# Fourier and hyena mixer products and filter spectra in one fp32 product on unsplit operands, with ordering conditions on the output products beside them

## The chip, the cores and the metric

The kernel runs on one core of one Trainium2 chip. The metric is the device time of one execution in microseconds (us), the median of several runs. TensorE does the matrix products (PE in the profile; its weight loads are PEld), VectorE (DVE) and ScalarE (ACT) the elementwise work, GpSimd (POOL) some of it, and SyncE (SP) issues most DMAs. Each engine executes its instructions in a fixed order.

## The reference, cut to what matters

The program computes two transformer layers, and then a further block with dilated and neighbourhood attention and a mixture of experts. Everything is fp32. The part that the change touches is in each of the two layers, on x (512 tokens) and, in layer 0 only, on the context c (256 tokens); width 1024, of which 512 go through attention, 256 through a Fourier mixer and 256 through a long convolution ("hyena"):

```
def fourier_mix(f, w):                       # f: B, L, 256 in 4 groups of 64
    y = jnp.fft.fft2(fg, axes=(1, 3), norm='ortho').real
    return y.reshape(B, L, FOURIER_W) @ w
def hyena_longconv(u, filt, bias):           # filt: 2L x 256, made by a small MLP, normalised
    uf = jnp.fft.rfft(u, n=2 * L, axis=1);  kf = jnp.fft.rfft(filt, n=2 * L, axis=0)
    y = jnp.fft.irfft(uf * kf[None], n=2 * L, axis=1)[:, :L]
    return y + u * bias
mix_x = jnp.concatenate([attn_x, four_x, hy_x], axis=-1) @ w_out[i]
```

The three FFTs (of the Fourier mixer, of the signal and of the filter) and the inverse one are products with tables of cosines and sines.

## The kernel before, in words

**The product in three.** Nearly all matrix products go through `mm3` (L306 to L312). Each operand is held as two tiles of the type fp32r, a high part and the rest, made by `split` (L334 to L338): ScalarE rounds into the high part (L337), VectorE or GpSimd subtracts (L338). `mm3` then issues three products: high times high (L310), high times low (L311), low times high (L312). In the trace each is one record. A few small products, the modulation vectors' (`mps`, L406) among them, take plain fp32 operands and are issued once; such a product shows as two records in the trace.

**The mixers.** `fourier` (from L1130) multiplies the 64-point table `bd` by the weight `wf` (tile `wps`, 4 products a layer), the strided columns of the signal `Fx` or `Fc` by that (`abps`, 512 columns each, 8 for x and 4 for c), and the result `ab` by the table `tf` (`yps`, 16 for x and 8 for c); VectorE adds the residues (`foac`, `foy`). `hyena` (from L1201) transposes the signal `u` (`utp`), multiplies by the table `hf` (`ups`, 8 for x, 4 for c), forms sums (`us`), multiplies by the filter's spectrum `kt` on VectorE and GpSimd, forms sums again (`zs`, then `zya` and `zyb`, which hold the spectrum Y), splits Y into `ys`, multiplies by the table `hi` (`iyp`, 16 for x, 8 for c) and scales and adds (`hyt`, L1305). In `yps` and `iyp` only 128 columns of most products are used; 256 are computed. Layer 0 thus has 4 + 12 + 24 + 12 + 24 = 76 such triple products, layer 1, without c, has 4 + 8 + 16 + 8 + 16 = 52.

**The filters.** `filters` (from L592) makes the filter of each layer and length. Its spectrum is `kps`, 40 triple products of 256 columns over the whole program (16 at the start, the others beside layer 0's attention), and an alternating sum `alt`, 20 products with four output rows.

**What sets the order.** The tile framework's scheduler writes a static order for each engine from the program and a model of times, so the code's generators give only a preference. `gated` (L509) adds a condition for that scheduler alone: an instruction is placed behind another; no semaphore comes of it. In layer 0 the Fourier mixer, hyena and `outA` (from L1506) are driven together: `outA` multiplies the attention's output `mixA` by the first half of `w_out` (tile `dps`, 4 blocks of x and 2 of c, 2 halves, 4 x 3 products each, so 144), writes it to DRAM (`yd`, L1518), from which it is read back as `y` (L1532). Then `outFH` multiplies the mixers' outputs (`mixF`, `mixH`) by the second half (again 144 products) and adds to `y`. The FFN follows. In layer 1 the mixers run beside the attention (`sps`, `ptp`, `po`), two steps of theirs to one of the attention.

**Loads.** The tables, and the signals that an earlier stage left in DRAM (`fd`), are loaded by `ldr` (L517) on GpSimd's queue, as fp32r; the signals of hyena (`u`, `x`, `x0uc`, L1209 to L1214) and the spectra `kt` by SP.

Of the kernel before, what the change touches and what calls it, by code (L numbers as in the profile page):

```python
# [27 lines left out]
def _split(v):  # L28
    v = np.asarray(v, np.float64)
    m, e = np.frexp(v)  # L30
    hi = np.ldexp(np.round(m * 4096.0) / 4096.0, e)
    r = v - hi
    m, e = np.frexp(r)
    lo = np.ldexp(np.round(m * 4096.0) / 4096.0, e)
    return hi.astype(np.float32), lo.astype(np.float32)


# [6 lines left out]
def consts():  # L44
# [17 lines left out]
    hf, hi = (np.stack(_split(np.stack(t, 1))).reshape(2, 128, 1024) for t in (hf, hi))  # L62
    c["hftab"], c["hitab"] = hf, hi
    tf = np.stack(_split(np.stack(tf, 1))).reshape(2, 128, 2, 768)
    c["ftab"] = tf.transpose(0, 2, 1, 3).reshape(4, 128, 768)
# [12 lines left out]
    c["bd64"] = np.stack(_split(bd), 0).transpose(2, 0, 1, 3).reshape(128, 512)  # L78
# [187 lines left out]
class Kern:  # L266
    def __init__(K, tc, A, off, out, dbg=None):
        K.tc, K.nc, K.A, K.off, K.out = tc, tc.nc, A, off, out
        K.dbg = dbg or {}
        K.n = 0  # L270
        K.bal = 0.0
        K.gate = None
        K.marks = []
# [76 lines left out]
    def setup(K):  # L350
# [11 lines left out]
        K.alt = K.cp.tile([128, 4, 4], F32R, name="alt")  # L362
        nc.vector.tensor_copy(K.alt.rearrange("p a b -> p (a b)"), K.sgn[:, 0:16])
# [228 lines left out]
    def filters(K, later, pg, hf=None):  # L592
# [21 lines left out]
        hf = list(hf or (K.ldr([128, 4, 2, 128], f"hf{p}", A["hftab"][p]) for p in range(2)))  # L614
        hn = pg([128, 2, 4, 1, 128], F32R, "hn")
        for p in range(2):
            nc.scalar.activation(hn[:, p, :, 0], hf[p][:, :, 1].bitcast(F32), AF.Copy, scale=-1.0)
            hf.append(hn[:, p])
# [21 lines left out]
    def filter(K, i, g, h2, w3, dec, hf):  # L640
# [4 lines left out]
        for b in range(nb):  # L645
            p3 = K.bank([128, 512], name="hp3")
            nc.tensor.matmul(p3, h2[:, b * 128:b * 128 + 128], w3, start=True, stop=True, tile_position=(64 * i, 0))
            fb = K.te([128, 2, 256], "hfb")
# [6 lines left out]
            kt = K.wlo([128, 2, 512], F32R, "kt")  # L655
            K.split(kt[:, 0], kt[:, 1], fb.rearrange("p a b -> p (a b)"))
# [4 lines left out]
            kts.append(kt)  # L661
# [76 lines left out]
    def mixer_in(K, i, pair, h, last, mods):  # L738
# [54 lines left out]
        for b in range(2):  # L793
            w = K.wk(K.wload(A["win"][i, 6 + b]), 128)
            for g in gs:
                n = 512 if g == "x" else 256
# [1 line left out]
                hi, lo = (K.te([128, 512], "fs", F32R)[:, :n] for p in range(2))
                K.split(hi, lo, ps)
                for p, t in enumerate((hi, lo)):  # L800
                    dst = K.fd[p, :, b * 512:b * 512 + 512] if g == "x" else K.fd[2, :, p * 512 + b * 256:p * 512 + b * 256 + 256]
                    nc.sync.dma_start(dst, t.bitcast(F32))
# [327 lines left out]
    def fourier(K, i, out, last, pg, t2):  # L1130

        nc, A = K.nc, K.A
        Fx = [K.ldr([128, 2, 512], f"Fx{p}", K.fd[p], pg) for p in range(2)]
        Fc = None if last else K.ldr([128, 2, 2, 256], "Fc", K.fd[2], pg)
        bd = K.ldr([128, 2, 2, 128], "bd", A["bd64"], pg)
        wf = t2([128, 2, 256], "wf")
        nc.sync.dma_start(wf.rearrange("p a b -> p (a b)"), A["wfour"][i])
        wr = pg([128, 2, 2, 256], F32R, "wr")
        K.split(wr[:, 0], wr[:, 1], wf)
        tf = [[K.ldr([128, 2, 384], f"tf{p}{j}", A["ftab"][2 * p + j], pg) for j in range(2)] for p in range(2)]  # L1140
        W = pg([128, 2, 512], F32R, "Wh"), pg([128, 2, 512], F32R, "Wl")
        for b in range(2):
            ps = K.bank([128, 2, 256], name="wps")
            for s in range(2):
                K.mm3(ps[:, s], (bd[:, 0, s], bd[:, 1, s]), (wr[:, 0, b], wr[:, 1, b]), True, True)
            ps = ps.rearrange("p a b -> p (a b)")
            K.split(W[0][:, b], W[1][:, b], ps)
        yield
        for g in (["x"] if last else ["x", "c"]):
            nb = 4 if g == "x" else 2  # L1150
            ab = []
            for r in range(nb):
                if r % 2 == 0:
# [1054 lines left out]
```

## Time and profile before

| | us |
|---|---|
| median of 3 runs | 2352.54 (2347.45 to 4198.28) |
| profiled execution, its own time | 2355.3 |
| its span | 2353.5 |
| TensorE busy | 2135.5 (91% of the span) |
| VectorE busy | 1522.3 (65%) |
| mean granted TensorE clock | 0.954 of full speed |

The stages in the span: the start with layer 0's filters and modulation to about 58 us, the input products to 170, attention 0 with the other filters to 362, the mixers of layer 0 with `outA` from 362 to 452.8, `outFH` to 485.5, then layer 0's FFN; attention 1 with layer 1's mixers from 1180 to 1321. The share of busy time is an average over all of these; what the change is worth is read from the stages that it touches, above all from the stretch from 362 to 453.

### The profile page before, as it was taken

The numbers are of one execution on the slowest core, as the hardware profiler recorded it, in microseconds if no ns is written. First come the engines' busy times: TensorE is split into PE (matmuls) and PEld (weight loads), VectorE is DVE, ScalarE is ACT, GpSimd is POOL, SyncE is SP. The second block draws the span as 40 slices with busy tenths as digits, with TensorE's granted clock in tenths as the row PEclk, the third lists the DMA queues.
The fourth block names the chain that finished last, engine by engine and source line by source line (L and its number), as shares of the span: only waits on it lengthen the run. The fifth ranks groups of instructions, "written<-read, shape, count | busy, mean of one in ns | idle before, by whom it ended". The sixth has DMA issues, their size and how long they took to land. (4 is left out here: it accounts for less than half of the span.)

```text
span 2353.5 us, 31469 instructions
## 1 busy us (share of the span) xinstructions
PE 2135.5 (91%) x11958; PEld 1744.1 (74%) x11958; DVE 1522.3 (65%) x2495; ACT 988.6 (42%) x1727; POOL 466.0 (20%) x448
## 2 busy tenths in 40 slices
PE   5899989679999999998987979999989999978895
PEld 2687678568888888886876768888867786756674
DVE  4744675777576777768557465555565645669895
ACT  3533663254322333235443444333344545347672
POOL 1410012221000000014213021000011212126743
PEclk9999999789999999999998989999999999979997
DMA  8363023623322344434130333222233335459993
GB/s 318 102 201 102 10 104 126 227 99 108 121 90 94 122 152 161 157 118 143 59 130 1 134 113 103 94 95 89 99 136 110 82 110 156 164 214 350 319 357 118
DMA packets 96991, 328.85 MB, mean 140 GB/s; under 512 B 11550, under 2 KB 12961, under 8 KB 96836
## 3 DMA queue, kind: packets, MB, share of 16 engines
q1 hardware_dynamic: 80176, 275.39, 33.0%
q0 software_dynamic: 14208, 42.48, 5.7%
q10 hardware_dynamic: 2452, 8.92, 0.9%
q8 instruction: 96, 1.57, 0.3%
q14 instruction: 59, 0.48, 0.1%
HBM read 285.68 MB, written 34.78 MB: 136 GB/s over the span
## 5 line engine op out<-in xcount | busy, mean ns | idle before, releaser
L328 DVE TENSOR_TENSOR wlo<-raw,whi 128x1024 fp32r<-128x1024 f32 x200 | 246.1, 1238 | 174.9 <-ACT whi L327 166.0
L327 ACT ACTIVATE whi<-raw 128x1024 fp32r<-128x1024 f32 x200 | 209.7, 1058 | 266.4 <-PE fps L311 196.6
L310 PE MATMUL fps<-h2x,whi 128*128 128x512 f32 x672 | 262.6, 392 | 4.0 <-DVE cvf L728 4.0
L311 PE MATMUL fps<-h2x,whi 128*128 128x512 f32 x672 | 263.0, 391 | 0.0
L312 PE MATMUL fps<-h2x,wlo 128*128 128x512 f32 x672 | 262.5, 391 | 0.0
L1413 POOL TENSOR_TENSOR cvf<-cvf 128x512 f32<-128x512 f32 x66 | 77.3, 1171 | 762.8 <-DVE cvf L728 681.9
L1336 DVE TENSOR_TENSOR y<-y,dps 128x512 f32<-128x512 f32 x200 | 134.2, 684 | 112.9 <-PE dps L312 112.4
L310 PEld LDWEIGHTS fps<-h2x,whi 128*128 128x128 f32 x672 | 126.5, 189 | 31.4 <-ACT whi L327 4.1
L312 PEld LDWEIGHTS fps<-h2x,wlo 128*128 128x128 f32 x672 | 126.9, 189 | 27.7 <-issue 1.6
L311 PEld LDWEIGHTS fps<-h2x,whi 128*128 128x128 f32 x672 | 127.0, 189 | 26.0 <-issue 0.4
L726 ACT ACTIVATE cvf<-fps,cv 128x512 f32<-128x512 f32 (+1 forms) x126 | 87.5, 695 | 138.6 <-PE fps L312 138.5
L311 PE MATMUL dps<-wlo,actx 128*128 128x512 f32 x352 | 137.1, 389 | 0.0
L310 PE MATMUL dps<-whi,actx 128*128 128x512 f32 x352 | 136.6, 390 | 0.3 <-DVE y L1336 0.3
L312 PE MATMUL dps<-whi,actx 128*128 128x512 f32 x352 | 136.3, 389 | 0.0
L429 DVE SCALAR_TENSOR_TENSOR ma<-wm,cs,ma 128x512 f32<-128x512 f32 x140 | 106.2, 803 | 19.3 <-DMA wm<-in_wmod 19.3
L310 PE MATMUL fps<-hx,whi 128*128 128x512 f32 x288 | 114.0, 396 | 0.5 <-ACT v L949 0.5
L312 PE MATMUL fps<-hx,wlo 128*128 128x512 f32 x288 | 113.3, 394 | 0.0
L311 PE MATMUL fps<-hx,whi 128*128 128x512 f32 x288 | 113.0, 392 | 0.0
L727 DVE SCALAR_TENSOR_TENSOR cvf<-fps,cv,cvf 128x511 f32<-128x511 f32 (+1 forms) x126 | 82.5, 655 | 30.5 <-ACT cvf L726 30.4
L310 PE MATMUL fps<-h2c,whi 128*128 128x256 f32 x336 | 96.3, 287 | 4.1 <-ACT cvf L726 4.1
L311 PE MATMUL fps<-h2c,whi 128*128 128x256 f32 x336 | 96.2, 286 | 0.0
L312 PE MATMUL fps<-h2c,wlo 128*128 128x256 f32 x336 | 96.2, 286 | 0.0
(630 smaller groups left out, 5514.5 us busy)
## 6 DMA issues: line engine op xcount, KB each, us to landing
wm<-in_wmod SPq DMA_DIRECT2D x96, 512.0 KB
raw<-in_wup SPq DMA_DIRECT2D x88, 512.0 KB
raw<-in_win SPq DMA_DIRECT2D x52, 512.0 KB
rawp<-in_wexp SPq DMA_DIRECT2D x48, 512.0 KB
raw<-in_wexp SPq DMA_DIRECT2D x48, 512.0 KB
raw<-in_wdown SPq DMA_DIRECT2D x44, 512.0 KB
raw<-in_wout SPq DMA_DIRECT2D x20, 512.0 KB
xd<-xt SPq DMA_DIRECT2D x20, 512.0 KB
```

Of the source, the lines that this page charges most:

```text
L310: mm(out, st[0], mv[0], start=start, stop=False)
L311: mm(out, st[0], mv[1], start=False, stop=False)
L312: K.lastmm = mm(out, st[1], mv[0], start=False, stop=stop)
L327: nc.scalar.activation(hi, raw, AF.Copy)
L328: (nc.gpsimd if pool else nc.vector).tensor_tensor(lo, raw, hi.bitcast(F32), op=ALU.subtract)
L429: o = nc.vector.scalar_tensor_tensor(a, v, c, a, op0=ALU.mult, op1=ALU.add)
L726: nc.scalar.activation(dst, ps, AF.Identity, scale=w[1], bias=w[3])
L727: nc.vector.scalar_tensor_tensor(dst[:, 1:n], ps[:, 0:n - 1], w[0], dst[:, 1:n], op0=ALU.mult, op1=ALU.add)
L1336: nc.vector.tensor_tensor(y[tb][:, c], y[tb][:, c], pss[hf], op=ALU.add)
L1413: nc.gpsimd.tensor_tensor(t[1], t[0], t[1], op=ALU.mult)
```

## The change

The Fourier and hyena products and the filter spectra are issued once each, in fp32, on unsplit operands (`mm1`, or `matmul` directly). The splits of those operands go: of `wf`, W, `ab`, `ut`, Y (the `ys` tiles), the filter (`kt`) and the signals (`fs`); where a copy from PSUM is still needed, one stays. The tables are held once instead of as two parts, and the loads of these operands move from GpSimd's queue to SP's (`ldf` for `ldr`). The columns that were computed and not used are dropped: `iyp` is 128 columns wide, `yps` 128 for c and for even residues of x. After it, layer 0 has 40 products of 128 columns, 24 of 256 and 12 of 512; layer 1 has 24, 20 and 8. The alternating sum takes four products at four column positions of the array. Last, in `outA`, the last product of each group is placed behind the mixer product that the program issued before the group began (`g = K.lastmm`, `K.gated(K.lastmm, g)`): a condition for the scheduler alone.

```diff
+    def mm1(K, out, st, mv, start, stop):
+        K.lastmm = K.nc.tensor.matmul(out, st, mv, start=start, stop=stop)
...
-    def ldr(K, shape, name, src, pg=None):
-
-        t = (pg or K.pg)(shape, F32R, name)
-        n = int(np.prod(shape[1:]))
-        flat = t if len(shape) == 2 else t.rearrange({3: "p a b -> p (a b)", 4: "p a b c -> p (a b c)", 5: "p a b c d -> p (a b c d)"}[len(shape)])
-        K.gated(K.nc.gpsimd.dma_start(flat, src))
+    def ldf(K, shape, name, src, pg=None):
+
+        t = (pg or K.pg)(shape, F32, name)
+        K.gated(K.nc.sync.dma_start(t if len(shape) == 2 else K.flat(t), src))
         return t
...
-            kt = K.wlo([128, 2, 512], F32R, "kt")
-            K.split(kt[:, 0], kt[:, 1], fb.rearrange("p a b -> p (a b)"))
...
-        alt = K.bank([128, 512], name="alt")[:nb]
+        alt = K.bank([128, 512], name="alt")
         for b, kt in enumerate(kts):
-            for z in range(2):
-                nc.tensor.matmul(alt, K.alt[:, b, :nb], kt[:, z], start=b == z == 0, stop=(b, z) == (nb - 1, 1))
-        ae = K.te([128, 512], "altr")[:nb]
-        nc.scalar.activation(ae, alt, AF.Copy)
+            nc.tensor.matmul(alt[32 * b:32 * b + 32], K.alt, kt.rearrange("p a b -> p (a b)"), start=True, stop=True, tile_position=(0, 32 * b))
+        ae = K.te([128, 512], "altr")[:32 * nb]
+        nc.scalar.activation(ae, alt[:32 * nb], AF.Copy)
...
-                    kv = tuple(kts[c][:, z, j * 256:j * 256 + 256] for z in range(2))
-                    K.mm3(ps[:, s], tuple(hf[z + 2 if t == 2 else z][:, c * (4 // nb), t % 2] for z in range(2)), kv, j == 0, j == 1)
+                    nc.tensor.matmul(ps[:, s], hf[t][:, c * (4 // nb)], kts[c][:, j], start=j == 0, stop=j == 1)
...
-        Fx = [K.ldr([128, 2, 512], f"Fx{p}", K.fd[p], pg) for p in range(2)]
-        Fc = None if last else K.ldr([128, 2, 2, 256], "Fc", K.fd[2], pg)
-        bd = K.ldr([128, 2, 2, 128], "bd", A["bd64"], pg)
-        wf = t2([128, 2, 256], "wf")
-        nc.sync.dma_start(wf.rearrange("p a b -> p (a b)"), A["wfour"][i])
-        wr = pg([128, 2, 2, 256], F32R, "wr")
-        K.split(wr[:, 0], wr[:, 1], wf)
-        tf = [[K.ldr([128, 2, 384], f"tf{p}{j}", A["ftab"][2 * p + j], pg) for j in range(2)] for p in range(2)]
-        W = pg([128, 2, 512], F32R, "Wh"), pg([128, 2, 512], F32R, "Wl")
+        Fx = K.ldf([128, 2, 512], "Fx", K.fd[0], pg)
+        bd = K.ldf([128, 2, 128], "bd", A["bd64"], lambda s, d, n: t2(s, n))
+        wf = K.ldf([128, 2, 256], "wf", A["wfour"][i], lambda s, d, n: t2(s, n))
+        Fc = None if last else K.ldf([128, 2, 256], "Fc", K.fd[2][:, 0:512], lambda s, d, n: pg([128, 4, 256], d, n)[:, 0:2])
+        tf = [K.ldf([128, 2, 384], f"tf{j}", A["ftab"][j], pg) for j in range(2)]
+        W = pg([128, 2, 512], F32, "W")
         for b in range(2):
             ps = K.bank([128, 2, 256], name="wps")
             for s in range(2):
-                K.mm3(ps[:, s], (bd[:, 0, s], bd[:, 1, s]), (wr[:, 0, b], wr[:, 1, b]), True, True)
-            ps = ps.rearrange("p a b -> p (a b)")
-            K.split(W[0][:, b], W[1][:, b], ps)
+                K.mm1(ps[:, s], bd[:, s], wf[:, b], True, True)
+            K.ev(W[:, b], ps.rearrange("p a b -> p (a b)"))
...
-                    st = tuple((Fx[z][:, b] if g == "x" else Fc[:, z, b])[:, r:r + nb * 127 + 1:nb] for z in range(2))
-                    K.mm3(ps, st, (W[0][:, b], W[1][:, b]), b == 0, b == 1)
-                K.split(tl[0][:, r % 2], tl[1][:, r % 2], ps)
-                ab.append((tl[0][:, r % 2], tl[1][:, r % 2]))
+                    K.mm1(ps, (Fx if g == "x" else Fc)[:, b, r:r + nb * 127 + 1:nb], W[:, b], b == 0, b == 1)
+                nc.scalar.activation(tl[:, r % 2], ps, AF.Copy)
+                ab.append(tl[:, r % 2])
...
+                        w = 256 if r % 2 and g == "x" else 128
                         for s in range(2):
-                            st = tuple(ab[r][z][:, s * 256 + ob * 128:s * 256 + ob * 128 + 128] for z in range(2))
                             c0 = 128 if s == 0 else 0
-                            mv = tuple(tf[z][cls // 2][:, cls % 2, c0:c0 + 256] for z in range(2))
-                            K.mm3(ps[:, j], st, mv, s == 0, s == 1)
+                            K.mm1(ps[:, j, 0:w], ab[r][:, s * 256 + ob * 128:s * 256 + ob * 128 + 128],
+                                  tf[cls // 2][:, cls % 2, c0:c0 + w], s == 0, s == 1)
...
-        hf = [K.ldr([128, 4, 2, 128], f"hf{p}", A["hftab"][p], pg) for p in range(2)]
-        hi = [K.ldr([128, 4, 2, 128], f"hi{p}", A["hitab"][p], pg) for p in range(2)]
+        hf, hi = (K.ldf([128, 4, 2, 128], n, A[n + "tab"], pg) for n in ("hf", "hi"))
...
-                K.split(ut[0][:, r], ut[1][:, r], ps)
+                nc.scalar.activation(ut[:, r], ps, AF.Copy)
...
-                        K.mm3(ps[:, s], (hf[0][:, cls, s], hf[1][:, cls, s]), (ut[0][:, r], ut[1][:, r]), True, True)
+                        K.mm1(ps[:, s], hf[:, cls, s], ut[:, r], True, True)
...
-            ys = [[pg([128, 2, 2, 256], F32R, f"ys{z}{j}") for j in range(nb // 2)] for z in range(2)]
-
-            for r in range(nb):
-                K.split(ys[0][r // 2][:, r % 2], ys[1][r // 2][:, r % 2], Y[r], nc.gpsimd if r % 2 else nc.vector)
...
-                        st = tuple(ys[z][r // 2][:, r % 2, s, cb * 128:cb * 128 + 128] for z in range(2))
-                        w = 128 if (cls == 3 and s == 1) else 256
-                        mv = tuple(hi[z].rearrange("p a b c -> p (a b c)")[:, cls * 256 + s * 128:cls * 256 + s * 128 + w] for z in range(2))
-                        K.mm3(ps[:, 0:w], st, mv, s == 0, s == 1)
+                        K.mm1(ps[:, 0:128], Y[r][:, s, cb * 128:cb * 128 + 128], hi[:, cls, s], s == 0, s == 1)
...
                                 ps = K.bank([128, 512], name="dps", tag="o")
+                                g = K.lastmm
                                 for k in range(4):
                                     K.mm3(ps, mixA.st(k, tb), (ws[k][0][:, c], ws[k][1][:, c]), k == 0, k == 3)
+                                K.gated(K.lastmm, g)
```

The order in which the engines now get their instructions differs at three places of weight. The first is TensorE in layer 0, from the end of the stretch before: `dps` with `mixA` is `outA`, `dps` with `mixF` is `outFH`. Before, all of `outA` stands ahead of the first `iyp`, and the transposes `utp` of c's signal `x0uc` and what follows have nothing between them and `outFH`:

```order
L312 MATMUL dps<-whi,mixAc_2014 128x512
L310 MATMUL iyp<-hi_3628,ys_3923 128x256
L311 MATMUL iyp<-hi_3630,ys_3923 128x256
...
L1227 MATMUL utp<-ident,x0uc 128x128 x4
L310 MATMUL ups<-ut_4116,hf_3624 128x256 x2
L311 MATMUL ups<-ut_4117,hf_3624 128x256
...
L310 MATMUL dps<-whi,mixFx_3547 128x512
```

Now 58 products of `outA` stand ahead of the first `iyp` (22 of them ahead of the first mixer product) and 86 behind it:

```order
L303 MATMUL iyp<-hi,zya 128x128 x2
L303 MATMUL iyp<-hi,zyb 128x128 x2
L303 MATMUL yps<-tf_3449,ab 128x128 x2
...
L300 MATMUL dps<-whi,mixAx_1948 128x512
...
L1206 MATMUL utp<-ident,x0uc 128x128 x4
L298 MATMUL dps<-whi,mixAx_1945 128x512
...
L303 MATMUL ups<-ut,hf 128x256 x4
...
L298 MATMUL dps<-whi,mixAc_1949 128x512
...
L303 MATMUL iyp<-hi,zya 128x128 x8
L298 MATMUL dps<-whi,mixFx_3405 128x512
```

What moved: the output products of attention now lie between the mixers' steps of hyena, and some 40 of them between `ups` and `iyp` of c.

The second is SP's queue in the same stage. Before, the load of `x0uc` stands behind all writes of `yd` and four loads of the FFN's weight (`raw<-in_wup`):

```order
L1518 DMA yd<-ya 128x1024 x4
L319 DMA raw<-in_wout 128x1024 x3
L1518 DMA yd<-ya 128x1024
L319 DMA raw<-in_wout 128x1024
L319 DMA raw<-in_wup 128x1024 x4
L1209 DMA x0uc<-fd_1335 128x1024
```

Now the eight loads from GpSimd's queue stand ahead of it, and it stands behind the second `yd` write:

```order
L519 DMA hi<-in_hitab 128x1024
L1192 DMA u<-fd_1283 128x1024
...
L1492 DMA yd<-ya 128x1024 x2
L1188 DMA x0uc<-fd_1283 128x1024
L1200 DMA kt_3802<-hyk_2520 128x1024
L1492 DMA yd<-ya 128x1024 x3
L310 DMA raw<-in_wout 128x1024 x3
L1492 DMA yd<-ya 128x1024
L310 DMA raw<-in_wout 128x1024
L310 DMA raw<-in_wup 128x1024
L1506 DMA y_3972<-yd 128x1024
```

What moved: `x0uc` forward past four writes and eight loads, three of the four `raw<-in_wup` back behind the reads of `y` and `x`.

The third is TensorE beside attention 1, between the last `ups` and the first `iyp` of layer 1. Before:

```order
L310 MATMUL ups<-ut_11052,hf_11036 128x256
L311 MATMUL ups<-ut_11053,hf_11036 128x256
L312 MATMUL ups<-ut_11052,hf_11038 128x256
L1121 MATMUL po<-pt_11346,vf 64x128 x4
L1110 MATMUL ptp<-ident,E 128x128 x8
...
L1121 MATMUL po<-pt_11531,vf 64x128 x4
L310 MATMUL iyp<-hi_11040,ys_11457 128x256
```

Now:

```order
L303 MATMUL ups<-ut,hf 128x256 x2
L1106 MATMUL po<-pt_10826,vf 64x128 x4
L1095 MATMUL ptp<-ident,E 128x128 x8
...
L1106 MATMUL po<-pt_11061,vf 64x128 x4
L303 MATMUL iyp<-hi,zya 128x128 x4
L303 MATMUL iyp<-hi,zyb 128x128 x4
L303 MATMUL iyp<-hi,zya 128x128 x4
```

What moved: between the two stood 2 groups of score products (`sps`), 20 transposes `ptp` and 32 products `po` of the attention; now there are 5 groups, 28 and 46.

## Rows read from the trace of the kernel before

**Rows 1.** The page, busy time: engine, busy us (share of the span), instructions.

```profile
PE 2135.5 (91%) x11958; PEld 1744.1 (74%) x11958; DVE 1522.3 (65%) x2495; ACT 988.6 (42%) x1727; POOL 466.0 (20%) x448
```

**Rows 2.** Windows, layer 0: end of the mixers with outA, iyp stage, outFH.

```profile
core 0: us, PE busy (x) PEld busy (x) DVE busy (x) ACT busy (x) POOL busy (x), PEclk, DMA share, GB/s
373.00:416.40 43.40, 43.40 (x238) 38.44 (x236) 31.29 (x65) 13.87 (x29) 11.02 (x9) 1.00 0.29 112
416.40:452.80 36.40, 18.36 (x102) 16.94 (x102) 30.91 (x63) 11.37 (x19) 8.55 (x7) 0.67 0.79 299
452.80:485.50 32.70, 32.70 (x146) 26.89 (x145) 16.73 (x24) 10.82 (x17) 6.64 (x4) 1.00 0.15 60
```

**Rows 3.** Waits of PE, 400 to 455: us in total, times, longest us.

```profile
PE iyp L310 <- ACT ys L337: 10.3, 3, 7.2
PE utp L1227 <- DMA x0uc<-fd: 5.3, 1, 5.3
```

**Rows 4.** Timeline of PE, triple products: start us, us, engine, line, tiles.

```profile
389.60 0.28 PE L310 MATMUL ups<-ut,hf 128*128 128x256 f32 x1
389.72 0.28 PE L311 MATMUL ups<-ut,hf 128*128 128x256 f32 x1
381.16 0.40 PE L312 MATMUL abps<-Wh,Fx 128*128 128x512 f32 x1
381.40 0.40 PE L310 MATMUL abps<-Wh,Fx 128*128 128x512 f32 x1
```

**Rows 5.** Timeline of PE, products on plain fp32 operands, and what came next.

```profile
43.66 2.80 PE L406 MATMUL mps<-wm,cs 128*32 128x256 f32 x48
46.39 0.38 PE L312 MATMUL kps<-kt,hf 128*128 128x256 f32 x1
51.87 1.05 PE L692 MATMUL fin<-sgn,hab 128*128 128x1 f32 x8
```

**Rows 6.** Tile kps, weight loads: duration ns least/median/most, starts, forms.

```profile
L310 PEld LDWEIGHTS kps<-kt,hf x30: 186/188/291, 35.3 to 328.6; 128*128 128x128 f32 x30
```

**Rows 7.** Timeline of SP's DMA issues (SPq), 368 to 433.

```profile
375.73 34.89 SPq L1518 DMA_DIRECT2D yd<-ya  x4
425.84 5.73 SPq L319 DMA_DIRECT2D raw<-in_wup  x4
431.69 0.43 SPq L1209 DMA_DIRECT2D x0uc<-fd  x1
```

**Rows 8.** DVE: hyena's first sum, its last before iyp, subtractions of ab.

```profile
393.66 0.68 DVE L1243 TENSOR_TENSOR us<-hue,ups 128x512 f32<-128x512 f32 x1
418.72 0.75 DVE L539 TENSOR_TENSOR zyb<-zs,zs 128x256 f32<-128x256 f32 x2
L338 DVE TENSOR_TENSOR ab<-abps,ab x10: 678/686/692, 388.6 to 1211.4; 128x512 fp32r<-128x512 f32 x10
```

**Rows 9.** Windows, layer 1: attention beside the mixers, and the iyp stage.

```profile
1180.00:1256.50 76.50, 66.16 (x555) 56.88 (x554) 51.06 (x107) 40.30 (x91) 8.86 (x14) 0.98 0.30 101
1256.50:1291.00 34.50, 18.62 (x125) 15.25 (x123) 28.48 (x41) 8.90 (x21) 19.62 (x16) 0.71 0.00 1
```

**Rows 10.** Waits of PE, 1170 to 1325, columns as in Rows 3.

```profile
PE iyp L310 <- ACT ys L337: 7.7, 1, 7.7
PE yps L310 <- DVE ab L338: 1.4, 1, 1.4
PE yps L310 <- DVE foac L1187: 1.1, 1, 1.1
```

**Rows 11.** Timeline of PE, one unit of attention 1, columns as in Rows 4.

```profile
1252.79 0.44 PE L1117 MATMUL po<-ident,rr 128*64 128x128 f32 x4
1254.04 0.66 PE L1110 MATMUL ptp<-ident,E 128*128 128x128 f32 x4
1254.45 0.48 PE L1093 MATMUL sps<-khx,qs 128*128 128x512 f32 x1
1255.23 0.40 PE L1093 MATMUL sps<-khx,qs 128*128 128x512 f32 x1
```

More of the change, by code (lines that the diff above doesn't have):

```diff
@@ L24 @@
 EPS = 1e-6
[L28 to L35, printed above, removed]
 def _linspace(a, b, n):
@@ L61, in consts @@
         tf.append(np.stack([s_, c_, -s_], 1))
[L62 to L65, printed above, removed]
+    c["hftab"], c["hitab"] = (np.stack(t, 1).reshape(128, 1024) for t in (hf, hi))
+    c["ftab"] = np.stack(tf, 1).reshape(128, 2, 768).transpose(1, 0, 2)
     h = np.where(n128 == 0, 0.5, 1.0)
@@ L77, in consts @@
         bd[1, g * 64:g * 64 + 64, g * 64:g * 64 + 64] = -np.sin(a) * sc
-    c["bd64"] = np.stack(_split(bd), 0).transpose(2, 0, 1, 3).reshape(128, 512)
+    c["bd64"] = bd.transpose(1, 0, 2).reshape(128, 256)
     zs, ds = [], []
@@ L271, in __init__ @@
         K.bal = 0.0
-        K.gate = None
+        K.gate = K.lastmm = None
         K.marks = []
@@ L361, in setup @@
         nc.sync.dma_start(K.sgn, A["sgn"])
-        K.alt = K.cp.tile([128, 4, 4], F32R, name="alt")
-        nc.vector.tensor_copy(K.alt.rearrange("p a b -> p (a b)"), K.sgn[:, 0:16])
+        K.alt = K.cp.tile([128, 32], F32, name="alt")
+        nc.gpsimd.memset(K.alt, 0.0)
+        nc.vector.tensor_copy(K.alt[:, 0:1], K.sgn[:, 0:1])
         K.hyrn = [[None, None], [None, None]]
@@ L590, in wlo, with filters @@
         return K.wp.tile(shape, dt, tag="wlo", name=name, bufs=K.NW)
-    def filters(K, later, pg, hf=None):
+    def filters(K, later, pg):
         nc, A = K.nc, K.A
@@ L613, in filters @@
             K.gated(nc.sync.dma_start(hx[64:128], K.h2d))
[L614 to L618, printed above, removed]
+        hf = K.ldf([128, 4, 2, 128], "hf", A["hftab"], pg)
+        hn = K.t2([128, 4, 128], "hn")
+        nc.scalar.activation(hn, hf[:, :, 1], AF.Copy, scale=-1.0)
+        hf = [hf[:, :, 0], hf[:, :, 1], hn]
         yield
@@ L647, in filter @@
             nc.tensor.matmul(p3, h2[:, b * 128:b * 128 + 128], w3, start=True, stop=True, tile_position=(64 * i, 0))
-            fb = K.te([128, 2, 256], "hfb")
+            if b % 2 == 0:
+                kt = K.wlo([128, 2, 2, 256], F32, "kt")
+            fb = kt[:, b % 2]
             nc.vector.tensor_tensor(fb, p3.rearrange("p (a c) -> p a c", a=2),
@@ L660, in filter @@
                 pa = ab
[L661 removed]
+            kts.append(fb)
             yield
[L663 removed]
+        alt = K.bank([128, 512], name="alt")
         for b, kt in enumerate(kts):
[L665 to L668 removed]
+            nc.tensor.matmul(alt[32 * b:32 * b + 32], K.alt, kt.rearrange("p a b -> p (a b)"), start=True, stop=True, tile_position=(0, 32 * b))
+        ae = K.te([128, 512], "altr")[:32 * nb]
+        nc.scalar.activation(ae, alt[:32 * nb], AF.Copy)
         yield
@@ L688, in filter @@
                 o = (2 * q + cb) * 128
-                nc.tensor.transpose(al[:, cb, q, :nb], ae[:, o:o + 128], K.ident[:nb, :nb])
+                nc.tensor.matmul(al[:, cb, q, :nb], ae[:, o:o + 128], K.ident[:32 * nb, 0:32 * nb:32], start=True, stop=True)
         for cb in range(2):
@@ L797, in mixer_in @@
                 ps = K.fm_prod(h, w, g)
[L798 to L802, printed above, removed]
+                t = K.te([128, 512], "fs")[:, :n]
+                K.ev(t, ps)
+                nc.sync.dma_start(K.fd[0, :, b * 512:b * 512 + 512] if g == "x" else K.fd[2, :, b * 256:b * 256 + 256], t)
                 run(2)
@@ L1153, in fourier @@
                 if r % 2 == 0:
-                    tl = [pg([128, 2, 512], F32R, f"ab{z}") for z in range(2)]
+                    tl = pg([128, 2, 512], F32, "ab")
                 ps = K.bank([128, 512], name="abps")
                 for b in range(2):
-                    st = tuple((Fx[z][:, b] if g == "x" else Fc[:, z, b])[:, r:r + nb * 127 + 1:nb] for z in range(2))
-                    K.mm3(ps, st, (W[0][:, b], W[1][:, b]), b == 0, b == 1)
-                K.split(tl[0][:, r % 2], tl[1][:, r % 2], ps)
-                ab.append((tl[0][:, r % 2], tl[1][:, r % 2]))
+                    K.mm1(ps, (Fx if g == "x" else Fc)[:, b, r:r + nb * 127 + 1:nb], W[:, b], b == 0, b == 1)
+                nc.scalar.activation(tl[:, r % 2], ps, AF.Copy)
+                ab.append(tl[:, r % 2])
                 if r % 2:
@@ L1222, in hyena @@
                 kt.append(t)
-            ut = [pg([128, 4, 256], F32R, f"ut{z}") for z in range(2)]
+            ut = pg([128, 4, 256], F32, "ut")
             for r in range(nb):
```

## The prediction

> **What bounds the kernel now.** I read the page's busy times first: TensorE is busy for 91% of the span [rows 1], so time can be won only where it waits or runs at the lower clock, or where it is given less to do. The table of windows then shows where that is. In the first of three windows of layer 0's mixers PE is busy throughout at full clock; in the second, from 416.4 to 452.8, it is busy for 18.36 of 36.40 us at a granted clock of 0.67 while VectorE is busy for 30.91; in the third, `outFH`, it is again busy throughout [rows 2]. All 144 products of `outA` were issued by 416.4 (the order shows them there), so nothing was left to lay beside hyena's chain on VectorE. The waits name the links: 10.3 us for the split of Y, and 5.3 us for the load of c's signal `x0uc` [rows 3]. That load's issue stands on SP behind writes of `yd` that took the queue 34.89 us and behind four loads of 512 KB that wait for buffers [rows 7]. In layer 1 the same chain shows: PE is busy for 18.62 of 34.5 us in the `iyp` stage, clock 0.71, and 66.16 of 76.5 before it [rows 9]; the longest wait is again Y's split, 7.7 us [rows 10].
>
> **The price of a product.** A triple product of 256 columns is three records spaced 0.12, so 0.36 us; of 512 columns, spaced 0.24, so 0.71 [rows 4]. For one fp32 product the nearest row is `mps`: 48 records, which are 24 products of 256 columns in six groups of four at different column positions, from 43.66 until the next product at 46.39, so 2.73 / 6 = 0.455 us a group [rows 5]. I take this as the time of one such product alone, hence 0.91 for 512 columns. For 128 columns half of it would be 0.23; the products of one column on full weights give 8 records in 1.05 us, that is 0.26 a product whatever its width [rows 5], so I take 0.24. Bounds: 0.24 from below for 256 columns, and above, the case that the weight loads do not hide, which is a rival below.
>
> Layer 0: 40 x 0.24 + 24 x 0.455 + 12 x 0.91 = 31.4 us, before 64 x 0.36 + 12 x 0.71 = 31.6. Layer 1: 24 x 0.24 + 20 x 0.455 + 8 x 0.91 = 22.1, before 44 x 0.36 + 8 x 0.71 = 21.5. Filters: 40 x 0.455 = 18.2, before 14.4; `alt` gives about 2 back (20 products of 512 at 0.24 = 4.8, now three groups of up to four at 0.91 = 2.7). So the work on TensorE stays what it was, within 3 us; what the narrower columns save, the fp32 passes cost. The whole gain has to come from waits.
>
> The row on weight loads bears on this price: a load of 128 columns takes 0.188 us [rows 6] while products on full weights follow each other every 0.12 [rows 4], so loads lie beside running products. The Trainium skill, page "TensorE: Matmul & The Clock Gate", section "The mechanism" of Part 3, says otherwise: a weight load overlaps running products only where it goes to other rows of the array. The trace of fp32r products disagrees with that; no row shows full-array fp32 products of some width. By the row the sum stays as above; by the rule it would be the third rival's.
>
> **Layer 0's mixers, -15 us.** The stage begins at 362 on PE. Now 58 products of `outA` at 0.227 (32.70 us for `outFH`'s 144 [rows 2]) = 13.2 stand ahead of the first `iyp`, with 4 `wps` 1.8, 12 `abps` 10.9, 8 `ups` 3.6, some 18 `yps` 6.1 and the transposes 1: 36.6 us, so PE is there at about 399. VectorE's chain sets Y. Its first `us` came at 393.66 and the last sum of Y ended at 418.72 + 0.75 = 419.47, 25.8 us later with VectorE saturated in between [rows 8]. Now the first two pairs of `ups` need 22 output products (5.0), `wps` 1.8, transposes 0.8, 8 `abps` 7.3 and 4 `ups` 1.8 ahead of them, 16.7 us, so 379; with the copy out of PSUM 379.5. Two subtractions of `ab` at 0.686 [rows 8] leave VectorE, but its other work beside the chain moves into the same stretch, so I keep 25.8: Y at 405.3, and the split of Y, which ended the 7.2 us wait, is gone. PE waits there for some 6 us. Behind that stand 86 output products 19.5, 24 `iyp` 5.8, 4 `yps` 1.0, 4 `ups` 1.8, transposes 0.4: 28.5 us. Some of it runs at the lower clock after the wait; I estimate 3.5 us, from the 0.67 of the window now [rows 2] and half as much idle time. `outFH` would begin at 405.3 + 28.5 + 3.5 = 437.3, before 452.8: -15. The wait for `x0uc` goes, since its load now stands behind the second `yd` write instead of the last; c's own chain lies beside 40 output products (9.1 us). Bounds: -24 if no wait is left (the 18.0 us idle in that window, and a third of the 18.4 busy ones for the clock); -5 if c's chain on VectorE is as long as it is now and leaves its own wait.
>
> The eight loads that come to SP's queue stand ahead of `u` there, and GpSimd's queue loses ten of them; the tables depend on nothing, the signals on the stage before, and each issue takes some 0.4 us [rows 7], 3.5 us in all, which lies within the 16.7 us before the first `ups`. I cost it at nothing; without that cover it is those 3.5 us. The dropped splits free ScalarE and VectorE, neither of which ends a wait at those places but for the chain above.
>
> **Attention 1 with layer 1's mixers, -9 us.** Between the last `ups` and the first `iyp` now stand three groups of scores, 8 transposes and 14 `po` more. A group of scores is 1255.23 - 1254.45 = 0.78, four transposes 0.41, ten `po` 1.25 [rows 11]: 2.3 + 0.8 + 1.75 = 4.9 us of the 7.7 are covered, and a split of Y of 0.7 goes too: -5.6. The wait of `yps` for the low part of `ab` goes, -1.4 [rows 10]; that for `foac` may stay. The split of `wf` ahead of the first product takes about 1 from VectorE's queue, on which attention's maxima wait: -0.5. The 16 `iyp` cost 0.36 - 0.24 = 0.12 less each, 1.9. Sum 9.4, taken as 9. The attention that is laid earlier is missing beside the rest of the `iyp` stage, so the least is -2; the most is -16, the 15.9 us in which PE idled there.
>
> **Filters and signals, 0.** The filters at the start lie beside the loads of the modulation's weights, those beside attention 0 in its gaps; they cost 3.8 - 2.1 = 1.7 us of PE. The splits of the signals (`fs`) shorten no wait that I see. 0, bounds -4 and +3.
>
> **The sum.** The profiled execution took 2355.3: 2355.3 - 15 - 9 = 2331.3. It stands 2.8 above the median of 2352.54, so the median would be **2328**, with 2314 to 2342 as this case's own range.
>
> **The rivals.**
>
> *The gain is given back to the loads.* In the window from 416.4 to 452.8 the core moved 299 GB/s [rows 2], 10.9 MB, for `outFH` and the FFN. If these cannot start earlier, because `raw` buffers come free no sooner and the last `yd` write, with `y`'s reads behind it, waits for the end of `outA`, then `outFH` or the FFN waits at its start for what layer 0 won. For it: the last `yd` write now stands near 436. Against: `outFH` needs one `y` block per 5.4 us, a quarter of that rate. Then layer 0 gives 3 and the time is 2355.3 - 3 - 9 - 2.8 = 2340.5.
>
> *All the idle time goes.* VectorE loses the splits, so Y may come when PE arrives; then layer 0 gives 24 and layer 1 gives 16 and the 10.3 idle of its first window: 2355.3 - 50.3 - 2.8 = 2302. Against: VectorE stays saturated between `us` and Y, and nothing there is shortened.
>
> *fp32 weight loads stay in view, and the kernel becomes slower.* An fp32 product has two records, so two loads; 168 products (76, 52 and 40) are 336 loads at 0.188 [rows 6], 63 us. About 19 of these would lie beside waits (6 at the first `iyp`, the rest at the start and in attention 0). Then 2328 + 44 = 2372. It decides from 24 / 336 = 0.07 us in view per load. Against: 8 records of one column on full weights take 1.05 us [rows 5], less than 8 x 0.188 = 1.5, so those hid.
>
> *The ordering does not bind.* The condition puts the last product of each group behind a mixer product in the order only; an engine that waits in order at the first `iyp` might idle as long as before. The order shows 86 products left for behind it, so this could only be if Y came 15 us later than I have it; then about 2343.
>
> **How the numbers follow.** Forecast 0.62; loads 0.17; all idle time 0.09; slower by loads of weights 0.08; ordering 0.04. The range of 2306 to 2350 holds the forecast, the loads and the ordering, and leaves out most of the other two. A measurement of this kernel can tell about 2%, 47 us: faster than 2305.5 has 0.08 (most of the second rival), slower than 2399.6 has 0.03 (the upper end of the third, were none of it hidden), within 0.89.
>
> **What would show it.** Right: `yps` and `iyp` of 128 columns spaced 0.24 at full clock, `abps` 0.9; one wait of PE for `zya` or `zyb` near 399 of about 6 us, none for `x0uc`; `outFH` beginning near 437; the `iyp` stage of layer 1 shorter by a quarter. Wrong: products of 256 columns spaced 0.7 or more at full clock; waits of PE for `raw` or `y` at the start of `outFH`; a first `us` later than 385, or more than 28 us from it to Y.

## The result: 0.987 of the time before, a little more than forecast

The changed kernel takes 2319.91 us in the median of four runs (2315.43 to 2323.86), against 2352.32 before: a ratio of 0.9869, with a 95% interval of 0.9842 to 0.9895. In a second comparison it took 2317.93 (0.9857, 0.9834 to 0.9879). The forecast was 2328, the range 2306 to 2350; the gain of 1.3% lies within the 2% to which I had given 0.89.

TensorE is busy for as long as before (2135.5 us [rows 1]); everything won is time in which it waited. The page of the changed kernel:

```profile
span 2322.1 us, 30979 instructions
PE 2134.9 (92%) x11802; PEld 1730.3 (75%) x11802; DVE 1493.1 (64%) x2453; ACT 972.8 (42%) x1698; POOL 443.8 (19%) x417
```

The windows of layer 0's mixers in the changed kernel, from the first product of `outA` to the first `iyp`'s wait, from there to `outFH`, and from `outFH` to the FFN's first product; they answer to [rows 2]:

```profile
core 0: us, PE busy (x) PEld busy (x) DVE busy (x) ACT busy (x) POOL busy (x), PEclk, DMA share, GB/s
354.80:392.50 37.70, 37.70 (x154) 29.58 (x154) 21.96 (x46) 11.11 (x24) 10.80 (x9) 0.95 0.20 78
392.50:432.20 39.70, 32.04 (x156) 26.88 (x155) 27.09 (x63) 10.72 (x20) 6.38 (x5) 0.91 0.34 124
432.20:469.10 36.90, 34.35 (x150) 27.70 (x150) 22.80 (x30) 13.43 (x22) 5.21 (x4) 0.98 0.88 335
```

In the stretch with `iyp` TensorE is now busy for 32.04 of 39.70 us at a granted clock of 0.91; before it was 18.36 of 36.40 at 0.67. The third stretch became longer by 2.4 us, and DMAs are now busy for 0.88 of it. PE's waits, 385 to 455, answer to [rows 3]:

```profile
PE iyp L303 <- issue: 5.0, 1, 5.0
PE dps L298 <- ACT ya L1490: 1.4, 3, 0.7
PE dps L298 <- DVE hyt L1277: 1.3, 1, 1.3
```

One wait is left at the first `iyp` (the row names no releaser; the first part of Y, `zya`, is ready at 396.92 + 0.68 = 397.60, below, and the product starts at 397.70), and that for `x0uc` is gone. The prices of one product show in PE's timeline, the chain in VectorE's (columns as in [rows 4]):

```profile
361.45 1.89 PE L303 MATMUL wps<-wf,bd 128*128 128x256 f32 x8
363.17 0.63 PE L1206 MATMUL utp<-ident,u 128*128 128x128 f32 x4
363.64 3.70 PE L303 MATMUL abps<-W,Fx 128*128 128x512 f32 x8
367.18 0.63 PE L1206 MATMUL utp<-ident,u 128*128 128x128 f32 x4
397.70 1.20 PE L303 MATMUL iyp<-hi,zya 128*128 128x128 f32 x4 [5.04 <-issue]
407.48 0.60 PE L303 MATMUL iyp<-hi,zya 128*128 128x128 f32 x4
407.92 0.61 PE L303 MATMUL iyp<-hi,zyb 128*128 128x128 f32 x4
428.70 2.22 PE L303 MATMUL iyp<-hi,zya 128*128 128x128 f32 x16
432.18 0.47 PE L298 MATMUL dps<-whi,mixFx 128*128 128x512 f32 x1 [1.26 <-DVE hyt L1277]
```

```profile
373.19 0.69 DVE L1222 TENSOR_TENSOR us<-hue,ups 128x512 f32<-128x512 f32 x1 [5.41 <-PE ups L303]
396.92 0.68 DVE L529 TENSOR_TENSOR zya<-zs,zs 128x512 f32<-128x512 f32 x1
398.46 0.75 DVE L529 TENSOR_TENSOR zyb<-zs,zs 128x256 f32<-128x256 f32 x2
```

Four products of 256 columns take 363.17 - 361.45 = 1.72, so 0.43 each (I had 0.455); four of 512 take 3.54, so 0.885 (0.91); two of 128 take 407.92 - 407.48 = 0.44, so 0.22 (0.24). The eight products of 128 at 428.70 take 1.95 us from the first start to the last, but a weight load among them waits 0.19 us for `hyt`, so that row is no price. From the first `us` to Y it is 398.46 + 0.75 - 373.19 = 26.0 us (25.8).

### The profile page after: what moved, and what is told of

Read it like the earlier page. It is cut to its first block, busy times and chain, and to the rows that moved or that the text cites. A ratio compares the mean times of both kernels' runs of the same rounds, so it can differ in the third digit from the quotient of the medians.

```text
span 2322.1 us, 30979 instructions
## 1 busy us (share of the span) xinstructions
PE 2134.9 (92%) x11802; PEld 1730.3 (75%) x11802; DVE 1493.1 (64%) x2453; ACT 972.8 (42%) x1698; POOL 443.8 (19%) x417
## 5 line engine op out<-in xcount | busy, mean ns | idle before, releaser
L298 PEld LDWEIGHTS fps<-h2x,whi 128*128 128x128 f32 x672 | 126.5, 189 | 31.4 <-ACT whi L318 4.1
```

## Where the time came from, stage by stage

The time of five stretches in the trace of each kernel, in us: to the first input product; from the first score of attention 0 to the first product of `outA`; from there to the first of `outFH`; from there to the FFN's first; from there to the last product of attention 1. The stretch between the first two is the same in all within 1 us.

| kernel | start | attention 0 | mixers 0 | outFH to FFN | FFN 0 to attention 1's end |
|---|---|---|---|---|---|
| before | 58.8 | 146.6 | 90.6 | 34.5 | 833.8 |
| changed | 55.8 | 142.4 | 77.4 | 36.9 | 824.2 |
| changed, again | 55.9 | 137.0 | 76.1 | 36.4 | 820.8 |
| order undone | 53.6 | 137.0 | 84.7 | 34.5 | 825.3 |
| order alone | 57.6 | 144.1 | 84.7 | 36.4 | 835.9 |
| filters undone | 57.6 | 141.8 | 75.3 | 36.4 | 824.5 |
| filters alone | 56.1 | 145.4 | 92.0 | 34.8 | 835.7 |
| layer 1 undone | 53.6 | 139.4 | 76.2 | 36.8 | 835.3 |
| wide fp32 | 52.4 | 136.9 | 77.4 | 42.0 | 824.9 |
| narrow fp32r | 57.5 | 143.4 | 90.9 | 39.4 | 831.3 |
| bd early | 56.2 | 136.9 | 76.0 | 36.3 | 826.2 |
| mod first | 55.5 | 139.3 | 76.4 | 37.4 | 817.7 |

The span of the changed kernel is 31.4 us shorter in its first profile: start -3.0, attention 0 -4.2, mixers -13.2, `outFH` to the FFN +2.4, layer 1 with the FFN ahead of it -9.6; 3.6 lie behind attention 1, where nothing was changed (that remainder varies by 8 us between these traces), and 0.2 in between.

Two things bear on how these columns are read. The last column holds layer 0's FFN and attention 1: in "wide fp32", "narrow fp32r" and "mod first", where the column before it is longest (42.0, 39.4, 37.4), the FFN up to layer 1's input products takes 587.0, 586.0 and 586.0 us, in the others 590.9 to 594.6, so there most of what one column loses the next gives back. And the start varies with the clock: in "order undone", "layer 1 undone" and "wide fp32" (52.4 to 53.6) the granted clock of the first 30 us is 1.00, in the other five traces with the new filters (55.5 to 56.2) 0.89 to 0.92, at the same order of TensorE's start. The changed kernel, and "order undone":

```profile
0.00:30.00 30.00, 16.09 (x79) 4.81 (x80) 13.56 (x26) 7.57 (x13) 4.03 (x12) 0.90 0.93 351
0.00:30.00 30.00, 15.42 (x90) 5.13 (x90) 14.30 (x27) 8.11 (x14) 4.72 (x13) 1.00 0.91 344
```

## The experiments

Times are medians; ratios are to the kernel before, run on the same chip, with 95% intervals. Several of these differ from the changed kernel by less than the intervals, so where a stage decides, its time in the table is the evidence; each of those is from one profiled execution.

**The order undone.**

```diff
                                     K.mm3(ps, mixA.st(k, tb), ...)
-                                K.gated(K.lastmm, g)
```

> The changed kernel without the condition on the output products. The order now has 132 of outA's 144 products ahead of the first iyp (58 in the changed kernel) and none behind c's ups. Theory (layer 0's gain comes from the output products laid beside hyena's chain): outFH begins some 14 us later than the 432.2 of the changed kernel, about 2334 us, with PE idle at the first iyp and again at c's. Rival (the fp32 products and the dropped splits carry it): 2320, as the changed kernel.

2323.37 us, 0.9895 (0.9868 to 0.9921). The mixers take 84.7, so 5.9 of the 13 to 15 us stay won without the condition. Its waits of PE, 395 to 440:

```profile
PE utp L1206 <- DMA x0uc<-fd: 7.5, 1, 7.5
PE iyp L303 <- DVE zya L1243: 6.5, 1, 6.5
PE iyp L303 <- issue: 1.9, 1, 1.9
```

Both of c's waits are back: for its signal, whose load again stands behind loads of weights, and for its spectrum, which nothing covers. So these two are what the condition takes away. But the whole rose by only 3 to 5 us over the changed kernel by the medians (6 to 9 by the ratios, whose intervals overlap), not 14: the mixers lose 7.3 to 8.6 us, 2 us come back at the FFN (34.5 for 36.9), and the condition carries about half, not all, of layer 0's gain.

**The order alone.**

```diff
                                 ps = K.bank([128, 512], name="dps", tag="o")
+                                g = K.lastmm
                                 for k in range(4):
                                     K.mm3(ps, mixA.st(k, tb), ...)
+                                K.gated(K.lastmm, g)
```

> The kernel before with nothing but the condition on the output products; all products stay three. The order has 58, 26 and 60 output products ahead of the first iyp, up to x0uc's transposes, and behind them, exactly as the changed kernel. Theory: layer 0 gains most of its 17 us, outFH begins between 436 and 441, about 2338 us; the rest of the gain (start, layer 1) is missing. Rival: 2352, since the splits of Y still stand between VectorE's chain and iyp and the wait only moves.

2345.85 us, 0.9974 (0.9963 to 0.9985). The mixers take 84.7 here too. With the very order of the changed kernel, and triple products, PE's waits from 395 to 450 are:

```profile
PE iyp L310 <- ACT ys L337: 8.3, 2, 7.8
PE yps L312 <- DVE ab L338: 0.8, 1, 0.8
PE iyp L312 <- DVE ys L338: 0.7, 1, 0.7
```

The wait for `x0uc` is gone, that for Y's split stays, 7.8 for 7.2, and `outFH` begins at 443.0, not between 436 and 441: the rival of this run had half the truth. Either half of the change alone takes 5.9 us off layer 0's mixers, both together 13.2 to 14.5. The products' share cannot be their work on TensorE, which is as long as before by the price of a product. I take it to be the splits that stood in VectorE's and ScalarE's chain, since the wait for Y's split is what stays here; no run keeps the splits beside single products, so this is argued and not shown.

**Layer 1's mixers undone.**

```diff
-                    yield from K.fourier(i, mixF, last, fpg, ft2)
+                    yield from K.fourier3(i, mixF, last, fpg, ft2)
-                    yield from K.hyena(i, mixH, last, fpg, ft2)
+                    yield from K.hyena3(i, mixH, last, fpg, ft2)
```

(`fourier3` and `hyena3` are those of the kernel before, with its tables, and layer 1's signal is written in two parts.)

> The changed kernel with layer 1's mixers in three products on split operands again (tables loaded on GpSimd's queue), layer 0 and the filters as changed. The order beside attention 1 is that of the kernel before (2 groups of scores, 20 transposes, 32 po between ups and iyp). Theory: the stage from attention 1 to its end gives its 10 us back, about 2330 us, and everything ahead of it is as in the changed kernel. Rival (the 10 us are a drift, not of the mixers): 2320.

2327.57 us, 0.9897 (0.9879 to 0.9915). The last column of the table goes back to 835.3. PE's waits from 1150 to 1300 are those of the kernel before within 0.3 us ([rows 10], and the second fence):

```profile
PE iyp L312 <- ACT ys L342: 7.7, 1, 7.7
PE ptp L1123 <- ACT E L1112: 6.8, 3, 5.4
PE po L1130 <- DVE pvf L1139: 5.7, 2, 4.3
```

```profile
PE ptp L1110 <- ACT E L1099: 7.1, 4, 5.3
PE po L1117 <- DVE pvf L1126: 5.8, 2, 4.3
PE iyp L310 <- DVE hyt L1305: 2.6, 4, 0.9
```

In the changed kernel, measured again, they are:

```profile
PE ptp L1095 <- ACT E L1084: 5.5, 6, 2.0
PE iyp L303 <- DVE hyt L1277: 4.8, 5, 2.6
PE wps L303 <- DMA bd<-in_bd: 3.4, 1, 3.4
PE iyp L303 <- DVE zya L529: 1.3, 1, 1.3
```

So the 9 to 10 us are layer 1's mixers' own: attention 1 alone, from its first score to `outA`, takes 143.0 us here, 142.1 in the kernel before, and 132.2 and 128.4 in the two profiles of the changed kernel. One new wait is among the latter's, for the table `bd`.

**The table bd earlier in layer 1.**

```diff
-        bd = K.ldf([128, 2, 128], "bd", A["bd64"], lambda s, d, n: t2(s, n))
+        bd = K.ldf([128, 2, 128], "bd", A["bd64"], lambda s, d, n: K.t2(s, n))
```

(and `wf` likewise)

> The changed kernel with bd and wf of layer 1 in the pool that is open from the start, not in the one that opens when the weights' buffers close. Theory: PE's wait of 3.4 us for bd ahead of layer 1's first product goes, about 2317 us; rival: the wait passes to Fx or to the first softmax, 2320.

2323.51 us, 0.9881 (0.9859 to 0.9903): no gain. The wait for `bd` is gone from the list, and that of the transposes for the softmax grew from 5.5 to 9.2:

```profile
PE ptp L1095 <- ACT E L1084: 9.2, 7, 3.0
PE iyp L303 <- DVE hyt L1277: 4.8, 5, 2.6
```

The wait passed to the softmax, as the rival had it. But the run does not isolate the load: the order moved too. In the changed kernel layer 1's first product stands behind two groups of scores, 5.0 us after the first score; here it stands behind five groups, 16 transposes and 14 `po`, 15.2 us after it.

**The filters undone, and the filters alone.** The first is the changed kernel with the filters of the kernel before, the second the reverse:

```diff
-                    nc.tensor.matmul(ps[:, s], hf[t][:, c * (4 // nb)], kts[c][:, j], start=j == 0, stop=j == 1)
+                    K.mm3(ps[:, s], tuple(hf[z + 2 if t == 2 else z][:, c * (4 // nb), t % 2] for z in range(2)), kv, j == 0, j == 1)
...
```

> The changed kernel with the filters of the kernel before (three products, split filter, the table in two parts on GpSimd's queue); mixers and order as changed. Theory (the start's 3 us come from the filters' loads and splits): the first input product begins near 58.8 and not 55.8, about 2323 us. Rival (the start is set by the loads of the modulation's weights alone): no change, 2320.

> The kernel before with the filters of the changed kernel alone (one fp32 product, unsplit filter and table, the table loaded by SP); mixers and their order as before. Theory (the step that I costed at nothing is worth 6 to 9 us): first input product 3.5 us earlier, attention 0 some 3 us shorter, nothing after that, about 2344 us. Rival (start and attention 0 vary by that much from run to run): 2351.

Undone: 2324.0 us, 0.9877 (0.9857 to 0.9898), the start 57.6 again. Alone: 2350.88 us, 0.9996 (0.9986 to 1.0007), the start 56.1, but attention 0 takes 145.4, and the whole is the same as before. The start is 57.5 to 58.8 in the four traces with the old filters and 52.4 to 56.2 in the eight with the new ones. So the filters are worth some 2 to 3 us at the start, more where the clock there is higher, and nothing that can be told from noise in the whole; my 6 to 9 were too much. The windows of attention 0 in the kernel before, the filters alone, the changed kernel and the changed kernel again:

```profile
215.60:362.20 146.60, 129.07 (x1054) 99.04 (x1053) 94.04 (x205) 88.13 (x206) 17.07 (x22) 0.94 0.21 74
```

```profile
213.10:358.50 145.40, 128.09 (x1038) 98.40 (x1037) 89.23 (x199) 84.61 (x199) 15.67 (x20) 0.94 0.21 71
```

```profile
212.40:354.80 142.40, 128.39 (x1039) 99.04 (x1037) 89.06 (x199) 84.70 (x199) 9.01 (x8) 0.94 0.15 51
```

```profile
213.20:350.20 137.00, 123.06 (x1038) 94.14 (x1036) 88.95 (x199) 84.63 (x199) 9.03 (x8) 0.99 0.14 50
```

The last two are one kernel: the same instructions, 14.0 us idle in both, and 5.4 us of difference with the granted clock, 0.94 or 0.99 of full speed (2.4 GHz). Idle time is 17.5 before and 17.3 with the filters alone, but 16.1 and 16.0 in "order alone" and "narrow fp32r", whose attention 0 is that of the kernel before, so 2 to 3.5 us are the kernel's. GpSimd is busy for 9 us in place of 16 to 17 where the mixers' tables are no longer loaded on its queue. Whether those loads are the cause was not tried by itself; with the filters undone, and those loads still gone, GpSimd is busy for 10.6 us and TensorE idle for 15.8.

**The changed kernel again.**

> The changed kernel once more, beside the others on their chip: 2320 us. For the stage times of its profile: if the stretches up to attention 0's end agree with the first profile within 2 us, the 8 us of the start and attention 0 are the kernel's; if they differ by 5, a part of it is the clock.

2317.93 us, 0.9857 (0.9834 to 0.9879). The start agrees within 0.1 us, attention 0 differs by 5.4. So of this profile's gain there, 9.6 us, more than half is the clock; the first profile's 4.2 cannot be explained by it, since its granted clock, 0.94, is that of the kernel before.

**The width of the products.** First the changed kernel with `iyp` and `yps` 256 columns wide in fp32, then the kernel before with both only as wide as used, in three fp32r products:

```diff
-                        w = 256 if r % 2 and g == "x" else 128
+                        w = 256
-                        K.mm1(ps[:, 0:128], Y[r][...], hi[:, cls, s], s == 0, s == 1)
+                        w = 128 if (cls == 3 and s == 1) else 256
+                        K.mm1(ps[:, 0:w], Y[r][...], hi.rearrange("p a b c -> p (a b c)")[:, ...], s == 0, s == 1)
```

> The changed kernel with iyp and yps computed 256 columns wide again, in fp32; nothing else. Theory (an fp32 product costs by its columns, 0.24 for 128 and 0.44 for 256): 40 products in layer 0 and 24 in layer 1 cost 0.2 more, 8 and 5 us; some 3 us of it lie in the wait at the first iyp, so about 2330 us. Rival (the weight loads set the spacing, whatever the width): 2320.

2327.07 us, 0.9901 (0.9883 to 0.9919).

```profile
368.86 3.62 PE L303 MATMUL yps<-tf,ab 128*128 128x256 f32 x16
```

Eight products of 256 columns in about 3.4 us: 0.43 each, against 0.22 for 128. The price is as I had it. The mixers' stretch grew by only 0 to 1 us: TensorE is idle for 4.8 us in it and not 7.2, and its granted clock is 1.00 and not 0.93 or 0.96. `outFH` to the FFN grew by 5, which the FFN gives back (587.0 us for 591.8 and 592.2). Layer 1 pays: attention 1 alone takes 136.2 for 132.2 and 128.4. The profiled execution is the fastest of five (2317.85), so most of the 7 to 9 us of the median cannot be found in this trace.

```diff
-                        w = 128 if (cls == 3 and s == 1) else 256
+                        w = 128
+                            w = 256 if r % 2 and g == "x" else 128
-                            mv = tuple(tf[z][cls // 2][:, cls % 2, c0:c0 + 256] for z in range(2))
+                            mv = tuple(tf[z][cls // 2][:, cls % 2, c0:c0 + w] for z in range(2))
-                            K.mm3(ps[:, j], st, mv, s == 0, s == 1)
+                            K.mm3(ps[:, j, 0:w], st, mv, s == 0, s == 1)
```

> The kernel before with iyp and yps only as wide as needed, still three fp32r products. If a fp32r product of 128 columns costs half of one of 256 (0.06), 64 triple products save 0.18 each, 11.5 us of PE work, part of it in waits: about 2345 us. If it costs the same (0.12, the weight load's pace), 2352. If it costs more than one of 256 columns, slower than 2352.

2356.01 us, 1.0016 (1.0006 to 1.0026).

```profile
387.80 0.27 PE L310 MATMUL yps<-tf,ab 128*128 128x128 f32 x1
387.91 0.27 PE L311 MATMUL yps<-tf,ab 128*128 128x128 f32 x1
388.54 0.28 PE L310 MATMUL yps<-tf,ab 128*128 128x256 f32 x1
388.66 0.28 PE L311 MATMUL yps<-tf,ab 128*128 128x256 f32 x1
```

A fp32r product of 128 columns follows the one ahead by 0.11 us, of 256 by 0.12: half the columns save nothing. A triple product of 128 columns is 0.33, a single fp32 one 0.22, so only the fp32 form profits from dropping columns. Why the kernel became 4 us slower stays open: the profiled execution is its fastest (2349.81) and does not show it.

**The modulation rows first.** The changed kernel's timeline shows VectorE waiting for a late load at the FFN's start:

```profile
455.92 1.23 DVE L1327 TENSOR_TENSOR y<-y,mod 128x1024 f32<-128x1024 f32 x1 [0.97 <-DMA mod<-md]
```

```diff
+        if i == 0:
+            K.G = K.grows(i, 0, False)
         K.xs = K.xload(tbs, i == 0)
-        K.G = K.grows(i, 0, i == 1)
+        if i == 1:
+            K.G = K.grows(i, 0, True)
```

> The changed kernel with the modulation rows (mod) loaded ahead of x and c at outFH's start. Theory (outFH to the FFN is 2.4 us longer than before since VectorE waits for mod until 455.9): that wait goes, outFH's begin to the FFN's first product takes 34.5 and not 36.9, about 2317 us. Rival (the y blocks or VectorE itself are late): 36.9 and 2320.

2312.73 us (2310.49 to 2313.83), 0.9831 (0.9816 to 0.9846): the fastest of all, 5 us under the changed kernel on the same chip, though the two intervals still overlap by a little. But not for my reason:

```profile
442.68 1.23 DVE L1327 TENSOR_TENSOR y<-y,mod 128x1024 f32<-128x1024 f32 x1
465.39 0.79 PE L298 MATMUL ups<-h2x,whi 128*128 128x256 f32 x2 [3.83 <-ACT h2x L500]
```

The addition of `mod` comes 13 us earlier, and yet `outFH` to the FFN takes 37.4: the wait passed to ScalarE's `h2x`. What is shorter is the last column (817.7), above all the FFN in it: 586.0 us for 591.8 and 592.2. VectorE now executes 36 instructions and not 30 ahead of the FFN's first product, and 637 and not 643 in the FFN, so a part of its work moved forward. No step of mine foresaw that, and no run isolates it.

## Why the prediction was right, and where it was not

**The price of the products held**: 0.43, 0.885 and 0.22 for 0.455, 0.91 and 0.24, and TensorE's busy time changed by 0.6 us. The third rival, weight loads in view, is ruled out. In the changed kernel the loads of `iyp` take, in ns (least/median/most):

```profile
L303 PEld LDWEIGHTS iyp<-hi,zya x48: 186/192/338, 397.7 to 1262.3; 128*128 128x128 f32 x48
```

A product of two records and two loads takes 0.22 us, less than two such loads behind one another. The Trainium skill's rule ("TensorE: Matmul & The Clock Gate", "The mechanism" of Part 3), that a load overlaps products only in other rows of the array, is contradicted by full-array fp32 products as well. The same section of the Trainium skill also has a load pulled ahead into a background weight buffer, and with that these rows agree.

**Layer 0's mixers: -15 forecast, -13.2 and -14.5 measured** up to `outFH`. The steps came as worked out: 5.0 us of wait at the first `iyp` (6), 26.0 from `us` to Y (25.8), 33.0 from there to `outFH` (32). All of it came 5 to 6 us earlier than my times, since `outA` began at 354.8 and not at 362. What failed is a reading behind the number: I named the order as what covers the waits; the two single runs show that the order alone wins 5.9 and the rest of the change without it 5.9, the latter, as I read it, by the dropped splits.

**The first rival may hold in small.** With the loads nearer together (DMA share 0.88, 335 GB/s, for 0.15 and 60 before [rows 2]), the FFN begins 2.4 us later after `outFH` than before, so 11 to 12.5 us are left of layer 0's gain. I had this as a case of its own and not as a part of the forecast. That the loads cause it is not shown: TensorE's waits there are 2.3 us for VectorE's `y`, and the one load that was moved forward, `mod`, did not shorten the stretch.

**Attention 1: -9 forecast, -9.6 measured** in the last column, -9.9 for attention 1 alone, where TensorE is idle for 18.3 us and not 29.0 (-11 in either as the mean of the kernels with each form, a part of it clock). The 4.9 us of covered wait were right in kind: 7.7 at the first `iyp` became 1.3. They were a little short, since the trace has 32 transposes between the last `ups` and the first `iyp` and not 28, 0.4 us more. But waits for `hyt` grew to 4.8 from 2.6, and one of 3.4 for `bd` is new, 5.6 us against me; and the attention's waits for `E` and `pvf` (7.1 and 5.8, now 5.5 and 1.0 to 1.2) fell by 6.2 to 6.4, which I had priced at 0.5. That these two nearly cancel is luck.

**The failed step is "Filters and signals, 0".** Its bounds were -4 and +3; the start and attention 0 gave -3.0 and -4.2, together -7.2, in the first profile. I costed the loads that moved to SP's queue at nothing and did not look at the order of the start: there 24 products of the modulation moved ahead of the filter's third product, and on SP's queue the loads of their weights (`wm`) no longer stand behind those of the input products (`raw<-in_win`). Before:

```profile
29.57 1.93 PE L406 MATMUL mps<-wm,cs 128*32 128x256 f32 x16
6.90 2.86 SPq L319 DMA_DIRECT2D raw<-in_win  x4
11.65 18.92 SPq L402 DMA_DIRECT2D wm<-in_wmod  x16
```

Now:

```profile
5.69 7.89 SPq L394 DMA_DIRECT2D wm<-in_wmod  x8
14.66 1.08 PE L398 MATMUL mps<-wm,cs 128*32 128x256 f32 x8 [6.27 <-DMA wm<-in_wmod]
```

That moved with the filters: the run with the filters alone starts its first such product at 14.98, that with the filters undone at 29.64. With the filters alone the two stretches gave 2.7 and 1.2, within my bounds; attention 0's other 3 us came only with the rest of the change, as TensorE's idle time at an equal granted clock (0.94), and no run says by which part of it.

**The number is nearer than its parts.** The sum for the profiled execution was 2331.3; with 7.2 less there, 4.2 more for layer 0 (-10.8 and not -15), 0.6 less for layer 1 and 3.8 less in stretches that I had not touched it is 2323.9, its own time. So 11.6 us that I had not forecast stand against 4.2 that did not come; that the forecast lies only 8 us off is partly luck.

## What to carry to other kernels

Price a change of number format by its columns: here one fp32 product of 128 columns beats three fp32r ones (0.22 against 0.33), at 256 they cost 0.43 against 0.36, so TensorE gains only where unused columns can go. The time was won in waits: by the order, and, as I read the runs, where splits left a saturated engine's chain. Where two measures serve one stretch, try each alone: here either won 5.9 us of layer 0's mixers, and neither one explains both. When loads change queues, read the order of every stage that they pass, not only of the one that uses them.

## What the runs showed of the hardware that I had not expected

The same instructions of attention 0 took 137.0 us at a granted clock of 0.99 and 142.4 at 0.94, in two profiles of one kernel with equal idle time; among the twelve traces this stretch is at 0.94 to 0.96 in eight and at 0.99 in four. The difference lies at its beginning: in the three windows of 10 us from 222 to 252 the slower profile has a granted clock of 0.83, 0.68 and 0.84, the other 1.00, 0.83 and 1.00, though TensorE is busy for nearly as long in both (7.9, 6.3 and 8.7 us; 7.4, 6.7 and 8.7). A fp32r product of 128 columns is no faster than one of 256 by more than a tenth (0.11 and 0.12 us), while a plain fp32 product costs by its columns: 0.22, 0.43 and 0.885 us for 128, 256 and 512.
